# A hybrid decoder layer in float32: a second gate-norm buffer, separate rings for two kinds of tiles, a scratch layout, and an exponential moved

## The chip, the cores and the metric

The kernel runs on one core of one Trainium2 chip. The metric is device time in microseconds of one execution; the times quoted are medians of repeated executions. One further execution was recorded by the hardware profiler; all views of the profile come from that one.

## The reference

One decoder layer (`DEPTH = 1`) works on 1104 token columns: 16 learned meta tokens, 1024 prompt tokens, and 8 sample sequences of 8 tokens. All of it is float32.

```
hn   = rmsnorm(h);  proj = hn @ w_in                       # 1024 -> 4112 columns
ya   = group_rmsnorm(gate_b * conv3(gate_c * hv))          # short convolution, 512 wide
xbc  = silu(conv4(xbc) + b);  xs, B, C = split(xbc)        # 1024 + 256 + 256
dt   = softplus(dt_raw + dt_bias);  a = cumsum(dt * A) per chunk of 128
y    = (C B^T * exp(a_l - a_s), causal) @ (x dt)  +  exp(a) * (C @ state)  +  D * xs
state= exp(a_end) * state + B^T @ (exp(a_end - a) * x dt)  # carried from chunk to chunk
yb   = group_rmsnorm(y * silu(z))                          # 2 groups of 512
h    = h + rmsnorm([ya, yb] @ w_out)
h    = h + rmsnorm((silu(fn @ w_gate) * (fn @ w_up)) @ w_down),  fn = rmsnorm(h)
```

The prompt is one meta chunk and eight chunks of 128; each sample sequence starts from its own recurrent state (8 x 2 x 8 x 64 x 128), which is read, updated and written.

## The kernel before

Every large product is done as three float32r matmuls on split operands (high x high, high x low, low x high). Weights are split on the fly: a transfer into `raw`, a copy on ScalarE (ACT) into the high part, a subtraction on VectorE (DVE) into the low part. `TT` numbers the token tiles: 0 is meta, 1 to 8 the prompt chunks, 9 the samples. Activations that are passed from stage to stage go through DRAM scratch tensors (`d_xbc`, `d_z`, `d_y`, `d_yb`, `d_ya`, `d_h`).

The stages are, in order of time: normalisation and transposes of x; the projections of x, B, C (`px`, until about 216 us); the chunked recurrence with the projections of z and of the short convolution woven between (`ssd_chunk`, `sample_state`, `finish`, `z_rows`, `sconv_rows`, until about 544 us); the output projection (L948 to L984, `o`); gate and up (L1005); down (L1346).

The kernel is written with a framework whose planner lays out each engine's instruction order at build time. It picks among what is ready by priority (program order, moved forward by `tc.high_priority`: 2000 for the chunks, 500 for `finish`, 200 for the samples) and by its own idea of durations; each engine then runs that order strictly, waiting on semaphores. All transfers are issued from the queue of SyncE (SP), in one order too, so a transfer that waits holds back those behind it. A tile with a `tag` has as many buffers as `bufs` says; a new tile of that tag waits until an older one's last reader is done. `po` is the pool of the recurrence; `pf` that of `finish`; `pm`, the pool of the output projection, takes over the memory of `po`: its loads come after the last instructions of `po` in the planned order (`p1.__exit__`, L784; `pmx`, L787).

What the change touches:

- `m_tile` (L384): 5 buffers of 4 KB per partition, tag `M`. They hold the decay matrices of a chunk (two per chunk, L507), the recurrent states of the samples (`s0`, L703, eight tiles, loaded by L706, written back by L728), and some small tiles (`dtmp`, `aT`, `xlo`).
- `y_of` (L483): `E` (one buffer) receives the cumulative log decays broadcast over 64 partitions from `d_a` (L495) and ACT takes the exponential of all of it (L497); DVE uses it in L527. `M` receives decays the same way (L508), has a per-partition value subtracted on DVE or ACT (L513, L516), the exponential on ACT (L517), and a product with `cb` on DVE (L518). `y` (one buffer) is started on ACT (L525) and stored into `d_y` (L539).
- `finish` (L541): loads `d_y` and `d_z` into `yf` and `zt` (one buffer each), gates, normalises, and stores into `d_yb` (L562). Chunk 8 is finished behind `po`'s end (`FIN[9]`, L785), the samples after the last projection (`LATE`).
- `load_mix` (L901): loads `d_yb` (`mrb`) and `d_ya` (`mra`), splits them on ACT (L914) and DVE, for three groups of three token tiles.
- L432 to L444: the cumulative log decays, transposed (`aT`, `aTs`), are stored into `d_a`.

Of the kernel before, what the change touches and what calls it, by code (L numbers as in the profile page):

```python
# [8 lines left out]
F32 = mybir.dt.float32  # L9
F32R = mybir.dt.float32r  # L10
# [6 lines left out]
P = 128  # L17
# [5 lines left out]
NS = 8  # L23
# [32 lines left out]
def hymba_kernel(ctx, tc, x_prompt, x_sample, state_sconv, state_ssm_conv, state_ssm, meta_tokens,  # L56
# [27 lines left out]
    d_xbc = dp.tile([12, P, T], F32, name="d_xbc")  # L84
    d_z = dp.tile([8, P, T], F32, name="d_z")
    d_ya = dp.tile([4, P, T], F32, name="d_ya")
    d_yb = {i: dp.tile([8, P, w], F32, name=f"d_yb{i}") for i, (_, w) in enumerate(TT)}
    d_y = {i: dp.tile([8, P, w], F32, name=f"d_y{i}") for i, (_, w) in enumerate(TT)}
    d_h = {i: dp.tile([w, DM], F32, name=f"d_h{i}") for i, (_, w) in enumerate(TT)}
    d_a = dp.tile([H, NCH + 1, P], F32, name="d_a")  # L90
    d_a2 = {n: dp.tile([P, NF // 2, 512], F32, name=f"d_a{n}") for n in (1, 2, 6, 7, 5, 4, 3)}
    d_fs = dp.tile([NF, 2, P, 32], F32, name="d_fs")
    d_t = dp.tile([P, 4, NF // 2, 512], F32, name="d_t")
# [288 lines left out]


    def m_tile(name):  # L384
        return po.tile([P, 8, P], F32, tag="M", name=name, bufs=5)

    NC2 = NCH + 2
    pd = ps.tile([P, NC2, H], F32, tag="small", name="pd", bufs=NSM)
# [4 lines left out]
        return po.tile([P, NC2, H], F32, tag="sc_" + name, name=name)  # L393

    dt, a_tok, a_end = sc("dt"), sc("a_tok"), sc("a_end")
    tmp = m_tile("dtmp")[:, :, :].rearrange("p j t -> p (j t)")
    t1, t2, t3, da = (tmp[:, q * NC2 * H:(q + 1) * NC2 * H].rearrange("p (c h) -> p c h", h=H) for q in range(4))
    wdt = po.tile([NMETA, 1, H], F32, tag="wdt", name="wdt")
    V.memset(dt, 0.0)
# [29 lines left out]
        V.tensor_tensor(out=e, in0=e, in1=a, op=ALU.subtract)  # L429
        S.activation(e, e, AF.Exp)  # L430
    V.tensor_tensor(out=wdt, in0=a_end[:NMETA, 0:1, :], in1=dt[:NMETA, 0:1, :], op=ALU.mult)
    aT = m_tile("aT")  # L432
    aTs = po.tile([H, NS * LS], F32, tag="soe", name="aTs")
    for c0, n in ((0, 4), (4, 4), (8, 1)):
        pa = ps.tile([P, 4, P], F32, tag="small", name=f"pa{c0}", bufs=NSM)
# [6 lines left out]
            V.tensor_copy(aTs, pa[:H, 0, :NS * LS])  # L442
    SY.dma_start(d_a[:, 0:NCH, :], aT[:H])
    SY.dma_start(d_a[:, NCH, 0:NS * LS], aTs)  # L444
    for j in (10, 11, 0, 1, 2, 3, 4, 5, 6, 7):
        st = xbc_begin(j)
        xbc_history(st)
        for t in range(3):
            xbc_tile(st, t, WIDE)
        xbc_end(st)  # L450
# [32 lines left out]
    def y_of(i, xb, bt, xd, off):  # L483

        t0, w = TT[i]
        c = i - 1
        smp = i > NCH
        if smp:
            E = po.tile([P, 8, NS * LS], F32, tag="ES", name="ES")
            y = po.tile([P, 8, NS * LS], F32, tag="yS", name="yS")  # L490
        else:
            E = po.tile([P, 8, P], F32, tag="E", name=f"E{i}")
            y = po.tile([P, 8, P], F32, tag="y", name=f"y{i}", bufs=YB)
        for e in range(2):
            SY.dma_start(E[64 * e:64 * e + 64, :, :w],  # L495
                         d_a[:, c, :w].rearrange("(j e) t -> e j t", e=2)[e].partition_broadcast(64))
        S.activation(E[:, :, :w], E[:, :, :w], AF.Exp)  # L497
        pcb = ps.tile([P, 2, P], F32, tag="small", name=f"pcb{i}", bufs=NSM)
        cb = po.tile([P, 2, P], F32, tag="cb", name=f"cb{i}")
        mask = U if w == P else Us  # L500
        for g in range(2):
            PE.matmul(pcb[:w, g, :w], xb[:, 8 + g, :w], xb[:, 10 + g, :w], start=True, stop=True)
        V.tensor_tensor(out=cb[:w, :, :w], in0=pcb[:w, :, :w], in1=mask[:w, :w].unsqueeze(1).to_broadcast([w, 2, w]),
                        op=ALU.mult)
        Ms = []
        for g in range(2):
            M = m_tile(f"M{i}{g}")  # L507
            SY.dma_start(M[:w, :, :w], d_a[8 * g:8 * g + 8, c, :w].partition_broadcast(w))  # L508
            mg = M[:w, :, :w]
            for h in range(8):  # L510
                a_s = a_tok[:w, i, 8 * g + h:8 * g + h + 1]
                if g == 0:
                    V.tensor_scalar(out=M[:w, h, :w], in0=M[:w, h, :w], scalar1=a_s, scalar2=0.0,  # L513
                                    op0=ALU.subtract, op1=ALU.min)
                else:
                    S.activation(M[:w, h, :w], M[:w, h, :w], AF.Relu, scale=-1.0, bias=a_s)  # L516
            S.activation(mg, mg, AF.Exp, scale=1.0 if g == 0 else -1.0)  # L517
            V.tensor_tensor(out=mg, in0=mg, in1=cb[:w, g, :w].unsqueeze(1).to_broadcast([w, 8, w]), op=ALU.mult)  # L518
            Ms.append(M)
        if not smp:  # L520
            po_ = big(f"po{i}")
            pov = po_.rearrange("p (j t) -> p j t", j=8)
            off(pov)
        for j in range(8):
            S.activation(y[:, j, :w], xb[:, j, :w], AF.Copy, scale=Dp[:, j:j + 1])  # L525
        if not smp:
            V.tensor_tensor(out=E, in0=pov, in1=E, op=ALU.mult)  # L527
        pd_ = big(f"pd{i}")
        pdv = pd_.rearrange("p (j t) -> p j t", j=8)
        for h in range(H):  # L530
            e = h % 2
            PE.matmul(pdv[64 * e:64 * e + 64, h // 2, :w], xd[:w, h * 64:(h + 1) * 64], Ms[h // 8][:w, h % 8, :w],
                      start=True, stop=True)
        if not smp:
            V.tensor_tensor(out=y, in0=y, in1=E, op=ALU.add)
        V.tensor_tensor(out=y[:, :, :w], in0=pdv[:, :, :w], in1=y[:, :, :w], op=ALU.add)
        if smp:
            return E, y
        SY.dma_start(d_y[i][:, :, :].rearrange("j p t -> p j t"), y)  # L539

    def finish(i):  # L541
        t0, w = TT[i]
        y = pf.tile([P, 8, P], F32, tag="yf", name=f"yf{i}")
        SY.dma_start(y[:, :, :w], d_y[i][:, :, :].rearrange("j p t -> p j t"))
        zt = pf.tile([P, 8, P], F32, tag="zt", name=f"zt{i}")
        SY.dma_start(zt[:, :, :w], d_z[:, :, t0:t0 + w].rearrange("j p t -> p j t"))
        yv = y[:, :, :w]
        V.tensor_tensor(out=yv, in0=yv, in1=zt[:, :, :w], op=ALU.mult)
        sq = zt
        S.activation(sq[:, :, :w], yv, AF.Square)  # L550
        sg = pf.tile([P, 2, P], F32, tag="sg", name=f"sg{i}")
        sv = sq[:, :, :].rearrange("p (g j) t -> p g j t", g=2)[:, :, :, :w]
        V.tensor_tensor(out=sv[:, :, 0:2], in0=sv[:, :, 0:2], in1=sv[:, :, 2:4], op=ALU.add)
        V.tensor_tensor(out=sg[:, :, :w], in0=sv[:, :, 0], in1=sv[:, :, 1], op=ALU.add)
        pn = ps.tile([P, 2, P], F32, tag="small", name=f"pn{i}", bufs=NSM)
        PE.matmul(pn[:, :, :w], ones, sg[:, :, :w], start=True, stop=True)
        S.activation(sg[:, :, :w], pn[:, :, :w], AF.Sqrt, bias=eps_c, scale=0.25 / 512)
        V.reciprocal(sg[:, :, :w], sg[:, :, :w])
        for g in range(2):
            yg = y[:, 4 * g:4 * g + 4, :w]  # L560
            V.tensor_tensor(out=yg, in0=yg, in1=sg[:, g, :w].unsqueeze(1).to_broadcast([P, 4, w]), op=ALU.mult)
        SY.dma_start(d_yb[i][:, :, :].rearrange("j p t -> p j t"), yv)  # L562

    def states(i, bt, xw):
        t0, w = TT[i]
# [120 lines left out]
    def sample_state(u, st):  # L686
# [13 lines left out]
                                in1=mk[h // w], op=ALU.mult)  # L700
            bms[0] = b1, b2
        b1, b2 = bms[0]
        s0 = m_tile(f"s0{u}")  # L703
        for q in range(2):
            rows = slice((j0 + q) * P, (j0 + q + 1) * P)
            SY.dma_start(s0[:, 4 * q:4 * q + 4, :], s_nat[b0:b0 + 4, rows, :].rearrange("b q n -> q b n"))  # L706
# [30 lines left out]
        V.tensor_tensor(out=t, in0=t, in1=E[:, j0:j0 + 2, tl], op=ALU.mult)  # L737
        V.tensor_tensor(out=y[:, j0:j0 + 2, tl], in0=y[:, j0:j0 + 2, tl], in1=t, op=ALU.add)
        if u == NS - 1:
            SY.dma_start(d_y[NCH + 1][:, :, :].rearrange("j p t -> p j t"), y)  # L740

    def conv_states():
        for q in range(2):
            pt = big(f"xlp{q}")
            for j in range(6):
                PE.transpose(pt[0:27, j * P:(j + 1) * P], xlast[:, 6 * q + j, :], ident)
            o = m_tile(f"xlo{q}")[0:27, :, :].rearrange("p j t -> p (j t)")[:, 0:6 * P]
            V.tensor_copy(o, pt[0:27, 0:6 * P])
            sl = slice(q * 6 * P, (q + 1) * 6 * P)
            SY.dma_start(o_xc_s[0].flatten_outer_dims()[:, sl], o[0:24, :])  # L750
            SY.dma_start(o_xc_p[0, 0][:, sl], o[24:27, :])
# [149 lines left out]
    def load_mix(part, tiles):  # L901
        nb = 8 if part == "b" else 4
        for i in sorted(tiles):
            t0, w = TT[i]
            raw = pm.tile([P, nb, P], F32, tag="mr" + part, name=f"mr{part}{i}", bufs=2)
            src = d_yb[i][:, :, :] if part == "b" else d_ya[:, :, t0:t0 + w]
            SY.dma_start(raw[:, :, :w], src.rearrange("j p t -> p j t"))
            mh = pm.tile([P, nb, P], F32R, tag="mh" + part, name=f"mh{part}{i}", bufs=4)
            if w == P:
                ml = pm.tile([P, nb, P], F32R, tag="ml" + part, name=f"ml{part}{i}", bufs=4)  # L910
                lo = ml
            else:
                ml, lo = None, mh[:, :, w:2 * w]
            S.activation(mh[:, :, :w], raw[:, :, :w], AF.Copy)  # L914
            minus(lo, raw[:, :, :w], mh[:, :, :w])
            mix[part, i] = mh, ml
# [496 lines left out]
```

## Time and profile before

| | us |
|---|---|
| median of 3 runs | 1437.35 (1436.61 to 1437.58) |
| profiled execution, its own time | 1438.31 |
| span of the profile | 1436.6 |
| TensorE (PE) busy | 1378.5, 96% of the span |
| VectorE (DVE) busy | 973.1, 68% |
| ScalarE (ACT) busy | 590.5, 41% |
| DMA queue of SP, 16 engines | 52.9% |
| granted TensorE clock, mean | 0.99 |

How to read it: the span begins with the first instruction of the profile and ends with the last; 1.7 us of the execution lie around it. PE is busy nearly everywhere, so what can be had or lost is the time in which PE waits and the time in which its clock is granted at half. The views name a line, an engine and tiles as `out<-in`.

### The profile page before, as it was taken

Reading aid. Unit: us, or ns where it says so; the run is one execution under the profiler, and the core shown is the slowest. Engines: PE = TensorE matmul, PEld = TensorE weight load, DVE = VectorE, ACT = ScalarE, POOL = GpSimd, SP = SyncE. Lnnn points to the kernel's source line nnn. Section 1 sums busy time; section 2 is a strip of 40 time slices with the busy share of each in tenths; the row PEclk is TensorE's granted clock in tenths of the full one; section 3 lists DMA queues with packets and bytes.
Section 4 is the critical chain, followed back from the end, with each engine's and each line's share of the span. In section 5 each row is a group of like instructions: output and inputs, shape, how many; then the busy total and the mean of one; then the engine's idle time right before and its main releaser. Section 6 shows DMA issues by size and latency. Waiting matters only on the chain.

```text
span 1436.6 us, 21982 instructions
## 1 busy us (share of the span) xinstructions
PE 1378.5 (96%) x8837; PEld 1254.4 (87%) x8837; DVE 973.1 (68%) x1321; ACT 590.5 (41%) x939; POOL 57.7 (4%) x110
## 2 busy tenths in 40 slices
PE   6999999989899996999998999999999999999997
PEld 5899998878798985887888999999999998888886
DVE  6455467776777888677489886667676666455565
ACT  5457444344443633466464222223322233443431
POOL 2011000000000000021010000000000000000001
PEclk9999999999999998999999999999999999999999
DMA  7135347666645557775535554443433468655454
GB/s 223 46 102 147 92 127 203 182 174 200 178 120 163 139 148 250 238 239 164 185 111 169 179 178 164 163 171 129 146 114 140 164 204 262 234 189 181 161 173 157
DMA packets 242190, 240.96 MB, mean 168 GB/s; under 512 B 34413, under 2 KB 195265, under 8 KB 242089
## 3 DMA queue, kind: packets, MB, share of 16 engines
q1 hardware_dynamic: 242088, 239.57, 52.9%
q8 instruction: 69, 1.13, 0.3%
q14 instruction: 33, 0.26, 0.1%
HBM read 170.81 MB, written 68.72 MB: 167 GB/s over the span
## 4 chain that ended last, share of the span: by engine, by line
PE 77%; DMA 8%; DVE 7%; ACT 4%; issue 2%; SPq 1%; POOL 0%; DVEq 0%; POOLq 0%; ACTq 0%
PE d L1346 14%; PE o L967 8%; PE yu L1005 7%; PE yg L1005 7%; PE zg L1005 5%; PE zu L1005 5%; PE xu L1005 4%; PE xg L1005 4%; DMA M<-d_a 3%; PE px L207 3%; PE px L209 3%; PE px L208 3%; PE pz L207 1%; DMA out_dram<-s 1%; PE pz L209 1%
## 5 line engine op out<-in xcount | busy, mean ns | idle before, releaser
L207 PE MATMUL px<-xh,whi 128*128 128x448 f32 (+2 forms) x288 | 95.5, 334 | 0.8 <-ACT xr L266 0.8
L208 PE MATMUL px<-xl,whi 128*128 128x448 f32 (+2 forms) x288 | 95.1, 331 | 0.0
L209 PE MATMUL px<-xh,wlo 128*128 128x272 f32 (+2 forms) x288 | 94.7, 332 | 0.0
L96 DVE TENSOR_TENSOR wlo<-raw,whi 128x1024 fp32r<-128x1024 f32 x32 | 39.1, 1221 | 52.3 <-ACT whi L102 45.1
L959 DVE SCALAR_TENSOR_TENSOR wol<-wo,vec,woh 128x1024 fp32r<-128x1024 f32 x36 | 46.1, 1281 | 37.9 <-ACT woh L958 37.9
L207 PE MATMUL pz<-xh,whi 128*128 128x256 f32 (+2 forms) x192 | 64.2, 334 | 2.9 <-DVE z L587 2.9
L209 PE MATMUL pz<-xh,wlo 128*128 128x256 f32 (+2 forms) x192 | 63.7, 332 | 0.0
L208 PE MATMUL pz<-xl,whi 128*128 128x256 f32 (+2 forms) x192 | 63.7, 332 | 0.0
L958 ACT ACTIVATE woh<-wo,vec 128x1024 fp32r<-128x1024 f32 x36 | 41.3, 1149 | 48.7 <-PE o L967 48.7
L239 DVE SCALAR_TENSOR_TENSOR xa<-xr,vec,xa 128x1128 f32<-128x1128 f32 x36 | 50.1, 1391 | 10.9 <-ACT xa L236 10.1
L207 PEld LDWEIGHTS px<-xh,whi 128*128 128x128 f32 x288 | 54.1, 188 | 3.1 <-ACT xr L266 1.0
L1346 PE MATMUL d<-wd,B01h 128*128 128x512 f32 x176 | 54.6, 390 | 2.2 <-ACT wd L1213 1.7
L209 PEld LDWEIGHTS px<-xh,wlo 128*128 128x128 f32 x288 | 54.1, 188 | 2.0 <-issue 0.2
L208 PEld LDWEIGHTS px<-xl,whi 128*128 128x128 f32 x288 | 54.1, 188 | 1.6
L102 ACT ACTIVATE whi<-raw 128x1024 fp32r<-128x1024 f32 x32 | 33.7, 1053 | 48.2 <-PE px L208 30.1
L967 PE MATMUL o<-woh,mhb 128*128 128x512 f32 x144 | 40.9, 407 | 11.8 <-ACT mhb L914 9.3
L967 PE MATMUL o<-wol,mhb 128*128 128x512 f32 x144 | 46.5, 409 | 2.3 <-DVE wol L959 1.9
L1346 PE MATMUL d<-wd,T3h 128*128 128x512 f32 x152 | 46.8, 389 | 0.0
L967 PEld LDWEIGHTS o<-woh,mhb 128*128 128x128 f32 x144 | 27.2, 194 | 19.6 <-ACT mhb L914 9.9
L1346 PE MATMUL d<-wd,T2h 128*128 128x512 f32 x144 | 44.2, 389 | 0.0
L1346 PE MATMUL d<-wd,B11h 128*128 128x512 f32 x144 | 44.0, 389 | 0.0
L967 PE MATMUL o<-woh,mlb 128*128 128x512 f32 x128 | 42.0, 407 | 0.0
(661 smaller groups left out, 4091.4 us busy)
## 6 DMA issues: line engine op xcount, KB each, us to landing
wo<-in_w_out_dram SPq DMA_DIRECT2D x36, 512.0 KB, 3.9
raw<-in_w_in_dram SPq DMA_DIRECT2D x32, 512.0 KB, 4.6
wg<-in_w_gate_dram SPq DMA_DIRECT2D x11, 1024.0 KB, 7.3
wu<-in_w_up_dram SPq DMA_DIRECT2D x11, 1024.0 KB, 6.6
xr<-in_w_down_dram SPq DMA_DIRECT2D x11, 1024.0 KB, 5.1
d_t<-xr SPq DMA_DIRECT2D x11, 1024.0 KB, 4.3
draw<-d_a SPq DMA_DIRECT2D x19, 512.0 KB, 5.0
xt<-in_x_prompt_dram SPq DMA_DIRECT2D x16, 512.0 KB, 5.3
```

The costliest lines, as they stand in the source:

```text
L96: V.tensor_tensor(out=out, in0=a, in1=hi.bitcast(F32), op=ALU.subtract)
L102: S.activation(hi[:, :], raw[:, :], AF.Copy)
L207: PE.matmul(acc, hi[:, wk], xh[t][:, k, o:], start=k == 0, stop=False)
L208: PE.matmul(acc, hi[:, wk], xl[t][:, k, o:], start=False, stop=False)
L209: PE.matmul(acc, lo[:, wk], xh[t][:, k, o:], start=False, stop=k == KD - 1)
L239: V.scalar_tensor_tensor(out=dst, in0=part(row, i), scalar=wv[:, wcol(i):wcol(i) + 1], in1=dst, op0=ALU.mult, op1=ALU.add)
L958: S.activation(hi, raw, AF.Copy, scale=nv)
L959: V.scalar_tensor_tensor(out=lo, in0=raw, scalar=nv, in1=hi[:, :].bitcast(F32), op0=ALU.mult, op1=ALU.subtract)
L967: PE.matmul(accs[i][c], l[:, kb, :], r_[:, c * 512:(c + 1) * 512], start=n == 0 and q == 0, stop=n == 11 and q == len(steps) - 1)
L1005: PE.matmul(acc[:, c, 0:W1], w_[l][k], b[r_][:, k, c * W1:(c + 1) * W1], start=start and k == 0 and x == 0, stop=k == 3 and x == 2, skip_g ...
L1346: PE.matmul(accs[t], sx[x][:, tl], wx[y], start=st and x + y == 0, stop=en and x == 1, skip_group_check=n not in OPENS)
```

## The change

It has four parts. (1) `finish` gets two `yf` buffers; to pay for it, the split short-convolution tiles of the output projection (`mha`, `mla`) get three instead of four. (2) The ring of five becomes `M` with three and `s0` with two; the samples' states and the small tiles go to `s0`. (3) `d_y` and `d_yb` are laid out `[128, 8, w]` instead of `[8, 128, w]`, so that a partition's row of a tile is one run in DRAM (4 KB for w = 128) and not eight runs of 512 bytes. (4) The exponential of the log decays is taken once on 16 partitions, stored into a new scratch tensor `d_e`, and `E` is loaded from there; L497 goes.

```diff
-    d_yb = {i: dp.tile([8, P, w], F32, name=f"d_yb{i}") for i, (_, w) in enumerate(TT)}
-    d_y = {i: dp.tile([8, P, w], F32, name=f"d_y{i}") for i, (_, w) in enumerate(TT)}
+    d_yb = {i: dp.tile([P, 8, w], F32, name=f"d_yb{i}") for i, (_, w) in enumerate(TT)}
+    d_y = {i: dp.tile([P, 8, w], F32, name=f"d_y{i}") for i, (_, w) in enumerate(TT)}
...
+    d_e = dp.tile([H, NCH + 1, P], F32, name="d_e")
...
     def m_tile(name):
-        return po.tile([P, 8, P], F32, tag="M", name=name, bufs=5)
+        return po.tile([P, 8, P], F32, tag="M", name=name, bufs=3)
+
+    def s_tile(name):
+        return po.tile([P, 8, P], F32, tag="s0", name=name, bufs=2)
...
-    tmp = m_tile("dtmp")[:, :, :].rearrange("p j t -> p (j t)")
+    tmp = s_tile("dtmp")[:, :, :].rearrange("p j t -> p (j t)")
...
-    aT = m_tile("aT")
+    aT = s_tile("aT")
...
     SY.dma_start(d_a[:, NCH, 0:NS * LS], aTs)
+    eT = s_tile("eT")
+    S.activation(eT[:H], aT[:H], AF.Exp)
+    S.activation(aTs, aTs, AF.Exp)
+    SY.dma_start(d_e[:, 0:NCH, :], eT[:H])
+    SY.dma_start(d_e[:, NCH, 0:NS * LS], aTs)
...
-                         d_a[:, c, :w].rearrange("(j e) t -> e j t", e=2)[e].partition_broadcast(64))
-        S.activation(E[:, :, :w], E[:, :, :w], AF.Exp)
+                         d_e[:, c, :w].rearrange("(j e) t -> e j t", e=2)[e].partition_broadcast(64))
...
-        SY.dma_start(d_y[i][:, :, :].rearrange("j p t -> p j t"), y)
+        SY.dma_start(d_y[i][:, :, :], y)
...
-        y = pf.tile([P, 8, P], F32, tag="yf", name=f"yf{i}")
-        SY.dma_start(y[:, :, :w], d_y[i][:, :, :].rearrange("j p t -> p j t"))
+        y = pf.tile([P, 8, P], F32, tag="yf", name=f"yf{i}", bufs=2)
+        SY.dma_start(y[:, :, :w], d_y[i][:, :, :])
...
-        SY.dma_start(d_yb[i][:, :, :].rearrange("j p t -> p j t"), yv)
+        SY.dma_start(d_yb[i][:, :, :], yv)
...
-        s0 = m_tile(f"s0{u}")
+        s0 = s_tile(f"s0{u}")
...
-            src = d_yb[i][:, :, :] if part == "b" else d_ya[:, :, t0:t0 + w]
-            SY.dma_start(raw[:, :, :w], src.rearrange("j p t -> p j t"))
-            mh = pm.tile([P, nb, P], F32R, tag="mh" + part, name=f"mh{part}{i}", bufs=4)
+            src = d_yb[i][:, :, :] if part == "b" else d_ya[:, :, t0:t0 + w].rearrange("j p t -> p j t")
+            SY.dma_start(raw[:, :, :w], src)
+            mh = pm.tile([P, nb, P], F32R, tag="mh" + part, name=f"mh{part}{i}", bufs=4 if part == "b" else 3)
...
-                ml = pm.tile([P, nb, P], F32R, tag="ml" + part, name=f"ml{part}{i}", bufs=4)
+                ml = pm.tile([P, nb, P], F32R, tag="ml" + part, name=f"ml{part}{i}", bufs=4 if part == "b" else 3)
```

Left out are the store of the samples' `y` (L740), changed as L539 is, and `xlo` (L747), moved to the second ring as `aT` is.

## Rows read from the trace of the kernel before

**Rows 1.** The page, part 1: busy us (share of the span) and instructions of each engine.
```profile
PE 1378.5 (96%) x8837; PEld 1254.4 (87%) x8837; DVE 973.1 (68%) x1321; ACT 590.5 (41%) x939; POOL 57.7 (4%) x110
```

**Rows 2.** Windows of 36 us: length, busy us of PE, PEld, DVE, ACT, POOL, then PEclk.
```profile
359.00:395.00 36.00, 31.17 (x240) 28.07 (x239) 28.68 (x43) 16.65 (x29) 0.00 (x0) 0.95 0.66 177
...
431.00:467.00 36.00, 35.39 (x227) 32.23 (x226) 26.78 (x29) 11.05 (x17) 1.08 (x2) 1.00 0.57 163
467.00:503.00 36.00, 36.00 (x241) 32.77 (x240) 32.14 (x49) 22.00 (x44) 1.65 (x2) 1.00 0.51 138
...
539.00:575.00 36.00, 25.10 (x102) 20.10 (x101) 29.20 (x29) 13.46 (x18) 0.56 (x1) 0.81 0.79 252
```

**Rows 3.** Waits of PE, 100 to 580 us: total us, times, longest us.
```profile
PE o L967 <- ACT mhb L914: 9.3, 1, 9.3
PE pcb L502 <- ACT bt L469: 4.8, 1, 4.8
PE pz L207 <- DVE z L587: 2.9, 2, 2.4
PE so L732 <- ACT s0t L713: 2.7, 2, 2.1
PE pd L532 <- DVE M L518: 1.4, 2, 1.2
...
PE so L732 <- ACT s0t L711: 0.9, 1, 0.9
```

**Rows 4.** Timeline of ACT: start us, us, instruction, [idle before it <- releaser].
```profile
242.24 1.07 ACT L497 ACTIVATE E<-E 128x1024 f32<-128x1024 f32 x1 [9.60 <-DVE M L513]
...
273.21 1.06 ACT L497 ACTIVATE E<-E 128x1024 f32<-128x1024 f32 x1 [6.40 <-DMA E<-d_a]
...
304.21 2.45 ACT L525 ACTIVATE y<-xb,Dp 128x128 f32<-128x128 f32 x8 [1.39 <-DVE s L725]
...
372.30 2.45 ACT L516 ACTIVATE M<-M,a_tok 128x128 f32<-128x128 f32 x8 [3.19 <-DMA M<-d_a]
```

**Rows 5.** Chain that ended last, in order of time: start us, us, what.
```profile
297.65 6.45 DMA d_y<-y
...
364.14 3.77 DMA out_dram<-s
367.98 4.21 DMA M<-d_a
...
540.74 5.92 DMA d_yb<-yf
...
547.75 6.24 DMA mrb<-d_yb
```

**Rows 6.** DMA issues by tile: count, KB each, median us to landing.
```profile
d_xbc<-xa SPq DMA_DIRECT2D x12, 520.0 KB, 2.7
...
d_y<-y SPq DMA_DIRECT2D x8, 512.0 KB, 6.5
```

**Rows 7.** Timeline of SP's queue, early and at the end of the recurrence.
```profile
97.17 0.38 SPq L443 DMA_DIRECT2D d_a<-aT  x1
...
541.33 0.39 SPq L759 DMA_DIRECT2D out_dram<-fso  x1
546.67 0.36 SPq L544 DMA_DIRECT2D yf<-d_y  x1
547.12 1.96 SPq L907 DMA_DIRECT2D mrb<-d_yb  x2
```

**Rows 8.** Windows at half clock, columns as in rows 2.
```profile
377.70:381.10 3.40, 3.29 (x16) 3.02 (x17) 2.04 (x4) 0.05 (x1) 0.00 (x0) 0.50 0.23 56
...
553.40:558.60 5.20, 5.13 (x12) 3.97 (x13) 4.33 (x7) 2.96 (x5) 0.00 (x0) 0.50 0.62 204
```

**Rows 9.** The samples' states: durations ns, first and last start us.
```profile
L706 SPq DMA_DIRECT2D s<-in_state_ssm_dram x16: 378/506/2268, 112.6 to 387.6; - x16
...
L728 SPq DMA_DIRECT2D out_dram<-s x16: 377/442/1108, 247.3 to 472.5; - x16
```

More of the change, by code (lines that the diff above doesn't have):

```diff
@@ L739, in sample_state @@
         if u == NS - 1:
-            SY.dma_start(d_y[NCH + 1][:, :, :].rearrange("j p t -> p j t"), y)
+            SY.dma_start(d_y[NCH + 1][:, :, :], y)
     def conv_states():
@@ L746, in conv_states @@
                 PE.transpose(pt[0:27, j * P:(j + 1) * P], xlast[:, 6 * q + j, :], ident)
-            o = m_tile(f"xlo{q}")[0:27, :, :].rearrange("p j t -> p (j t)")[:, 0:6 * P]
+            o = s_tile(f"xlo{q}")[0:27, :, :].rearrange("p j t -> p (j t)")[:, 0:6 * P]
             V.tensor_copy(o, pt[0:27, 0:6 * P])
```

## The prediction, made before the result was known

> **What bounds the kernel now.** I read the page's first part, then windows of equal length, the waits of PE, and for each wait the timelines of ACT and SP and the chain. PE is busy 96% of the span [rows 1], so its matmuls are the floor, and none of them changes: only idle time of PE, and time at half clock, can be won. The change touches the stretch from about 100 to 580 us. There the longest wait is 9.3 us, before the first matmul of the output projection; inside the recurrence lie waits of 4.8, 2.9, 2.7, 1.4 and 0.9 us, together 12.7 [rows 3]. Two of the longer waits are followed by a stretch at half clock (0.50, that is 1.2 of 2.4 GHz): 3.3 us of matmuls after the 4.8 us wait, 5.1 after the 9.3 us one [rows 8]. Work at half clock takes twice as long, so these cost about 1.65 and 2.55 us. What the change could win is then at most 12.7 + 1.65 = 14.35 us in the recurrence and 9.3 + 2.55 = 11.85 at its end, 26 together. The reader is also to see how busy DVE is: 28.7 us of 36 in the window of the 4.8 us wait, 32.1 of 36 just after 467 us, where PE has no idle at all [rows 2]. DVE's work does not shrink either.
>
> **Where each wait comes from, and what each part does to it.**
>
> *Separate rings.* In the chain the store of a sample's new state (3.77 us from 364.14) is followed at once by the load of an M (4.21 us from 367.98) [rows 5]: that M took the buffer that the sample's state was leaving. ACT, whose next instruction is the subtraction on this M, idles 3.19 us for it and starts at 372.30 [rows 4]; behind it stand its 2.45 us and one more exponential, and only then the copy `bt` for which PE waits 4.8 us. Without the store in front, the load starts some 3.8 + 0.4 us earlier (the store, and its issue, priced as the 0.38 us of rows 7), so the wait shrinks by 4.2 and its half clock (1.65) goes. The 1.4 us wait for M's product on DVE comes from the same order one step earlier, and I take 1.2 of it. Direct shift: 4.2 + 1.65 + 1.2 = 7.05 us. Ends: 0, if another wait is right behind, and 4.8 + 1.4 + 1.65 = 7.85.
>
> *Exponential of E gone from ACT.* ACT stood idle 9.60 us before the E exponential at 242.24 and 6.40 before that at 273.21 [rows 4]. The first is put down to DVE, but what it reads is the load of E; either way, copies of projections queue behind it, and PE's 2.9 us (longest 2.4) is for `z`, which such a copy feeds. With L497 gone ACT passes on. I take 2.35 of the 2.4 and half of the 0.9 for `s0t`, which follows the second: 2.8 us; ends 0 and 3.3. The wait does not vanish: it moves to DVE's L527, which reads E. Behind L527 in DVE's queue stand the sums into `y` and the splits of weights; it also needs PE's product with the state. If E were as late there as it was for ACT, the 2.8 would be lost. ACT also saves 9 exponentials of up to 1.07 us, worth nothing on an engine that is busy 41% [rows 1].
>
> *y in tile order.* Starting `y` on ACT waits for the store of the last `y`, which lands 297.65 + 6.45 = 304.10 [rows 5]; ACT starts it at 304.21 for 2.45 us [rows 4], and behind it come the `s0t` copies for which PE waits 2.7 [rows 3]. Stores of rows of 512 bytes land after 6.5 us; a store of nearly the same size in long rows, `d_xbc`, after 2.7 [rows 6]. So the store lands up to 3.8 us earlier; I take 2.5 us off PE's wait, since an exponential of M stands before it in ACT's queue. Ends: 0 and 2.7. Loads in long rows may gain too; I put them at nothing. The Trainium skill speaks against this part: "DMA: Bandwidth & Descriptors", Specifications, has runs of 512 bytes already at line rate. By that rule the 2.5 us would be nothing and the sum below 1.5 smaller; no run so far has this tile in long rows, and the two stores above differ by far more than their size.
>
> The direct shifts sum to 7.05 + 2.8 + 2.5 = 12.35 us. I take 60% of it, 7.4: the whole order is laid out anew, and DVE, 28.7 to 32.1 us of 36 [rows 2], has to do the same work in the shorter stretch. The ends stay 0 and 14.35.
>
> *Two yf buffers.* At the end of the recurrence the gated chunk 7 is stored (540.74, landing after 5.92 us) [rows 5]. Chunk 8's load into the one `yf` waits in SP's queue for that landing and is issued at 546.67; directly behind it, at 547.12, go the first loads of the output projection, which need nothing of chunk 7 or 8 [rows 7]. The instruction before them, the store of the final state, was issued at 541.33. With a second buffer chunk 8's load goes right behind (0.39), the projection's loads (0.36 later) at about 542.1: 5.0 us earlier. PE's wait becomes 9.3 - 5.0 = 4.3 us: the final state must still go through PE and ACT before `pm` opens, and the load itself takes 6.24 [rows 5]. A 4.8 us wait left 3.3 us of matmuls at half clock [rows 8], so I keep 1.65 of the 2.55: 0.9 more. Together 5.9; ends 0 (the loads wait for something else of `po`) and 11.85. Late next is that same load and its split.
>
> *What is added.* Two exponentials on 16 partitions (no longer than 1.07 each), two stores (0.38 each in SP's queue), and the first E load, behind these, waits for one of them to land (2.7, as a store of rows 6): some 1.07 + 0.38 + 2.7 = 4.2 us in SP's queue near 100 us, in front of weights for the projections. These are loaded ahead, and PE has no wait of size there (its long ones in rows 3 are later); I put it at 0, ends 0 and 4.2. `mha` and `mla` with three buffers: a group uses three; the fourth only let one split go early. A full-size operation is 1.07 us on ACT [rows 4], half of that for these tiles, and PE works a whole group between load and use: 0, ends 0 and 2.
>
> M with three: the M of the next chunk's second half can be loaded only when this chunk's first eight heads are multiplied. Load 4.21, subtraction 2.45, exponential about 1.06: 7.7 us, against some 36 us from chunk to chunk (the recurrence's last store at 541.33 less the first store of a state at 247.3, over eight) [rows 7, 9]. The old ring was not really wider: eight states were loaded by 387.6 and the last stored at 472.5 [rows 9], so that late in the recurrence states held buffers of the five for long; yet PE lost only 0.6 us of the 36 from 431 [rows 2]. I put it at 0; if its cover is gone, 7.7 a chunk. Two s0 buffers: a state waits for the store of the last but one, a chunk or so back: nothing, or one landing of 3.77.
>
> **Sum.** 7.4 + 5.9 = 13.3 us. The profiled execution took 1438.31 us, so 1425.0; it lies 1.0 above the median of the timed runs, 1437.35, which I take as the base: 1437.35 - 13.3 = 1424.
>
> **The rivals.**
>
> *One half alone.* The recurrence gains nothing that lasts, since DVE then sets the pace, and only the 5.9 us at its end come: 1431.5; the other way round (7.4 alone) 1430. For it: DVE's 32.1 of 36 us. Against: PE's waits lie where DVE had 7 us free.
>
> *Nothing comes of it.* The new order puts another wait where the old ones were (chunk 8's gate, final state), or the loads do not move since they waited for memory of `po`: 1437. For it: all these waits end at transfers of 4 to 6 us, and the planner puts instructions where it believes transfers to be done. Against: at 546.67 and 547.12 nothing but the buffer was in the way.
>
> *Slower: the ring of three.* The planner believes loads to be quick and puts the next chunk's second M right where PE needs it; then ACT and DVE stand at M's load in each chunk, with the fills' copies behind them, as ACT did at 372.30. Of the 7.7 us a third reaching PE in each of 8 chunks is 20.5 us: 1437.35 - 13.3 + 20.5 = 1444.5. It decides from 13.3 / 8 = 1.7 us of PE's wait per chunk. For it: the samples' two M's hold two of the three until their products, so the second M of chunk 1 starts late. Against: rows 2 and 9, as above.
>
> **How the numbers follow.** Forecast 0.55, one half alone 0.20, nothing 0.11, slower 0.14. The measurement can tell 0.2%, 2.9 us, from no change; so faster 0.75, same 0.11, slower 0.14. The likeliest case alone runs from 1414 (nearly all of 26 us) to 1430. The range of 1413 to 1440 takes in the second and third case and leaves out most of the slower one, and little below.
>
> **What would show it.** Right: no ACT instruction on E; loads of M no longer behind a sample's store, and no wait of PE for `bt` or `z` over 1 us; `d_y` landing in 3 to 4 us; the output projection's first loads issued within 1 us of the final state's store, with PE's wait there near 4 us; PE's busy sum the same but for the half clock. Wrong: PE waiting for M or for DVE in most chunks; `E` ending DVE's waits at L527; the first projection load still held by SP's queue.

## The result, and the profile after

The changed kernel takes 1421.42 us (median of 5 runs, 1419.32 to 1423.27) beside 1437.58 us for the kernel before measured with it. The ratio is 0.988, with a 95% interval of 0.9861 to 0.9898: faster by 1.2%, some 16 to 17 us. The forecast was 1424, in a range of 1413 to 1440. The profiled execution took 1421.42 us, with a span of 1419.7.

The engines of the page, as in [rows 1]:

```profile
PE 1376.9 (97%) x8837; PEld 1254.7 (88%) x8837; DVE 972.7 (69%) x1321; ACT 582.9 (41%) x932; POOL 66.1 (5%) x110
```

PE has the same 8837 matmuls and nearly the same busy time. So the 16.9 us of span can lie only in idle time of PE and in time at half clock, and windows cut at the stages say where. First the kernel before, then the changed one; the columns are those of [rows 2], and the stages are the recurrence up to the first matmul of the output projection, then output projection, gate and up, and down.

```profile
216.00:553.40 337.40, 314.41 (x2178) 279.56 (x2176) 261.72 (x352) 141.37 (x256) 7.80 (x16) 0.99 0.61 170
553.40:721.70 168.30, 163.04 (x710) 131.30 (x710) 113.79 (x129) 90.21 (x124) 14.10 (x12) 0.96 0.65 210
721.70:1196.80 475.10, 468.94 (x3721) 467.26 (x3722) 345.08 (x502) 157.79 (x246) 5.00 (x6) 1.00 0.46 158
1196.80:1436.60 239.80, 230.11 (x1014) 189.65 (x1012) 134.17 (x168) 90.30 (x125) 6.68 (x9) 0.99 0.58 195
```

The changed kernel:

```profile
216.00:534.00 318.00, 309.77 (x2151) 275.15 (x2150) 259.50 (x350) 137.95 (x259) 15.83 (x15) 0.99 0.62 179
534.00:700.20 166.20, 161.13 (x736) 131.93 (x735) 114.00 (x130) 87.99 (x123) 15.52 (x14) 1.00 0.65 213
700.20:1178.40 478.20, 471.53 (x3722) 469.59 (x3722) 345.96 (x502) 158.63 (x246) 5.01 (x6) 0.99 0.46 157
1178.40:1419.70 241.30, 231.71 (x1014) 190.74 (x1012) 134.28 (x168) 90.49 (x125) 6.68 (x9) 0.98 0.58 193
```

The length of a window less PE's busy time is PE's idle time. Of a stretch at half clock, half of its matmul time counts as lost. The lengths alone would mislead, because 26 matmuls have moved from the recurrence into the output stage (x2151 for x2178, x736 for x710). By stage, in us:

| stage | idle before | idle after | half clock before | half clock after |
|---|---|---|---|---|
| up to the end of `px` (216) | 14.0 | 13.2 | 0 | 0 |
| recurrence, without the wait for `mhb` | 13.8 | 8.2 | 1.6 | 1.6 |
| wait for `mhb` [rows 3] | 9.3 | 0 | | |
| output projection | 5.3 | 5.1 | 6.0 | 0 |
| gate and up | 6.2 | 6.7 | 1.7 | 4.5 |
| down | 9.7 | 9.6 | 0 | 1.7 |

Four sums follow. The waits inside the recurrence shrank by 5.6. At its end 9.3 + 6.0 + 0.2 = 15.5 went. The two last stages gave 4.9 back (0.5 of idle time less 0.1, and 2.8 + 1.7 of half clock). The first stage gained 0.8. Together 17.0, the difference of the spans (16.9) but for rounding.

All of this is read from one execution of each kernel. The kernel before, timed again beside the experiments, took between 1432.79 and 1444.25 us at mean granted clocks of 0.987 to 0.993, so a few us of half clock in a stage may belong to the execution and not to the kernel.

PE's waits between 100 and 580 us, the four longest; to be held against [rows 3]:

```profile
PE so L740 <- ACT s0t L721: 2.6, 1, 2.6
PE pb L208 <- DVE gc L631: 2.3, 1, 2.3
PE ph L208 <- DVE u L618: 1.5, 2, 1.2
PE pz L208 <- DVE z L595: 1.5, 1, 1.5
```

The waits for `mhb` and for `bt` are gone. The longest near the end is now one of 2.3 us in the short-convolution rows, for `gc`. SP's queue at that place, to be held against [rows 7]:

```profile
522.06 0.39 SPq L767 DMA_DIRECT2D out_dram<-fso  x1
522.54 0.53 SPq L963 DMA_DIRECT2D wo<-in_w_out_dram  x1
523.46 0.79 SPq L570 DMA_DIRECT2D d_yb<-yf  x1
524.30 1.72 SPq L915 DMA_DIRECT2D mrb<-d_yb  x2
```

The final state's store is 19.3 us earlier than before (522.06 for 541.33), and the projection's first loads follow it after 2.2 us instead of 5.8 (547.12). The chain that ended last, from that load on, answers to the end of [rows 5]:

```profile
524.30 6.23 DMA mrb<-d_yb
...
530.55 1.07 ACT mhb L922
```

The load is no faster than before (6.23 for 6.24). What differs is what PE has to do meanwhile, in a window from the final state's transposes to the first `o`:

```profile
520.00:534.00 14.00, 13.65 (x83) 12.60 (x82) 13.54 (x18) 5.75 (x7) 0.06 (x1) 1.00 0.76 228
```

PE is busy for 13.65 of 14.00 us. Of the projections woven into the recurrence, 72 matmuls stand in the timeline between these transposes and the first `o` and 48 more behind it; in the kernel before it was 24 and 24, and then 9.30 us of nothing. The early final state is for the greater part work moved behind it, not time won. The windows from the start to the last of its transposes, before and after:

```profile
0.00:539.73 539.73, 512.00 (x3370) 462.10 (x3371) 368.65 (x514) 249.59 (x444) 31.96 (x83) 1.00 0.53 149
0.00:520.70 520.70, 499.59 (x3297) 450.54 (x3298) 365.66 (x508) 240.00 (x434) 38.80 (x81) 1.00 0.54 155
```

Of the 19.0 us between them, 12.4 are matmuls that now come later (512.00 less 499.59); 6.6 are idle time less.

### The profile page after: what moved, and what is told of

The parts are those of the page before. It is cut to its first block, busy times and chain, and to the rows that moved or that the text cites. A ratio compares the mean times of both kernels' runs of the same rounds, so it can differ in the third digit from the quotient of the medians.

```text
span 1419.7 us, 21974 instructions
## 1 busy us (share of the span) xinstructions
PE 1376.9 (97%) x8837; PEld 1254.7 (88%) x8837; DVE 972.7 (69%) x1321; ACT 582.9 (41%) x932; POOL 66.1 (5%) x110
## 4 chain that ended last, share of the span: by engine, by line
PE 56%; DVE 3%; DMA 2%; ACT 1%; issue 1%; POOL 0%; SPq 0%; DVEq 0%; POOLq 0%; ACTq 0%
PE d L1354 14%; PE o L975 9%; PE yu L1013 7%; PE yg L1013 7%; PE zg L1013 5%; PE zu L1013 5%; PE xg L1013 4%; PE xu L1013 4%; DMA mrb<-d_yb 1%; PE d5s L1365 1%; PE d1s L1365 1%; PE fT L899 1%; DMA drawbh<-in_w_down_dram 0%; DMA d_a<-f 0%; DMA yf<-d_y 0%
## 5 line engine op out<-in xcount | busy, mean ns | idle before, releaser
L524 ACT ACTIVATE M<-M,a_tok 128x128 f32<-128x128 f32 (+1 forms) x72 | 21.8, 384 | 52.8 <-DMA M<-d_a 52.8
L1354 PEld LDWEIGHTS d<-wd,B01h 128*128 128x128 f32 x176 | 33.6, 192 | 10.0 <-ACT wd L1221 2.1
```

The lines of the kernel that those rows point to most:

```text
L1354: PE.matmul(accs[t], sx[x][:, tl], wx[y], start=st and x + y == 0, stop=en and x == 1, skip_group_check=n not in OPENS)
```

## The experiments

All ran beside the kernel before, in five rounds. The changed kernel was timed apart from the others, so all are compared by their ratio to before; "gain" is one minus that ratio, times 1437.58. "Left" counts the projections' matmuls still to come at the final state's transposes, before plus after the first `o`. By the intervals a gain is known to some 2 to 4 us. A profile shows one execution: that of `only_exp`, 1439.58 us, was the longest of twelve.

| kernel | median us | ratio (95%) | gain us | left |
|---|---|---|---|---|
| changed kernel | 1421.42 | 0.988 (0.9861 to 0.9898) | 17.2 | 72 + 48 |
| `no_yf` | 1434.39 | 0.9973 (0.9958 to 0.9989) | 3.9 | 24 + 0 |
| `no_ring` | 1426.02 | 0.991 (0.9891 to 0.9929) | 12.9 | 24 + 24 |
| `no_lay` | 1426.18 | 0.9911 (0.989 to 0.9931) | 12.8 | 72 + 48 |
| `no_exp` | 1425.3 | 0.9914 (0.9895 to 0.9933) | 12.4 | 72 + 48 |
| `only_yf` | 1428.69 | 0.9923 (0.9896 to 0.995) | 11.1 | 24 + 24 |
| `only_ring` | 1437.64 | 0.9989 (0.9971 to 1.0007) | 1.6 | 24 + 0 |
| `only_lay` | 1434.6 | 0.9975 (0.996 to 0.9991) | 3.6 | 24 + 24 |
| `only_exp` | 1434.21 | 0.9967 (0.9954 to 0.9981) | 4.7 | 24 + 0 |
| `yf_ring` | 1429.79 | 0.9945 (0.9929 to 0.9962) | 7.9 | 72 + 48 |
| `b_fill` | 1438.26 | 1.0002 (0.9989 to 1.0016) | -0.3 | 48 + 24 |
| `pool_yf` | 1431.5 | 0.9965 (0.9947 to 0.9982) | 5.0 | 24 + 24 |
| `a_fill` | 1426.25 | 0.9928 (0.9906 to 0.9949) | 10.4 | 72 + 48 |

**One part taken out of the changed kernel.**

`no_yf`: one `yf` buffer again, and four of `mha` and `mla`.

```diff
-        y = pf.tile([P, 8, P], F32, tag="yf", name=f"yf{i}", bufs=2)
+        y = pf.tile([P, 8, P], F32, tag="yf", name=f"yf{i}")
...
```

> The changed kernel with one yf buffer again (and four buffers for the split short-convolution tiles). Theory A (each part removes its own wait, as the prediction priced them): chunk 8's load into yf waits again for the store of chunk 7 and holds the output projection's first loads; PE's wait before that projection comes back, 5.9 us lost: 1427.3 against 1421.4. Theory B (the parts do not stand for themselves: the planner lays the whole order anew and the gain is a property of that order): within 2 us of the changed kernel, or off by an amount with no wait of PE behind yf in the trace.

Measured: 13.3 us of the 17.2 are lost. SP's queue at the end of the recurrence:

```profile
546.79 0.39 SPq L767 DMA_DIRECT2D out_dram<-fso  x1
547.75 0.32 SPq L552 DMA_DIRECT2D yf<-d_y  x1
548.13 1.37 SPq L915 DMA_DIRECT2D mrb<-d_yb  x2
```

The queue does not hold the projection's loads here for long (1.34 us behind the final state's store). The final state itself is 24.7 us later than in the changed kernel (546.79 for 522.06). And PE does not wait for `mhb`, but for the short convolution:

```profile
PE pb L208 <- DVE gc L631: 5.9, 2, 5.3
```

So here the second buffer is worth more than twice the 5.9 us of the prediction, and not by the stall on SP's queue alone: with it the planner ends the recurrence earlier, in part by leaving more projections behind it (120 for 24).

`no_ring`: one ring of five for both.

```diff
-        return po.tile([P, 8, P], F32, tag="M", name=name, bufs=3)
+        return po.tile([P, 8, P], F32, tag="M", name=name, bufs=5)
     def s_tile(name):
-        return po.tile([P, 8, P], F32, tag="s0", name=name, bufs=2)
+        return m_tile(name)
```

> The changed kernel with one ring of five for M, states and small tiles again. Theory A: loads of M stand again behind stores of the samples' states; ACT waits for them with copies for PE behind, 4.2 us lost (the priced 7.05 at 60%): 1425.6, at most 1428.5. Theory B: no such rise; ACT waits for M in either kernel, and PE has projections to do meanwhile: 1420 to 1423.

Measured: 4.3 us lost. The expected size comes out, but by another way: PE waits 2.0 us for `bt`, and 3.7 for `mhb`, since only 24 matmuls are left to cover that load.

`no_lay`: `d_y` and `d_yb` as `[8, P, w]`, with the rearranged views, at all five places.

```diff
-        SY.dma_start(d_y[i][:, :, :], y)
+        SY.dma_start(d_y[i][:, :, :].rearrange("j p t -> p j t"), y)
...
```

> The changed kernel with y and yb in DRAM as eight blocks of 128 partitions again (runs of 512 bytes). Theory A: stores of y land later again and ACT's start of the next y with them: 1.5 us lost, 1422.9. Theory B: the store is not on PE's path in the new order: 1421.4 within 1 us, with only the landings of d_y and d_yb longer.

Measured: 4.4 us lost; neither size fits. The landings stand further below.

`no_exp`: `E` from `d_a`, with the exponential on ACT, and without the five lines on `eT` and `d_e`.

```diff
-                         d_e[:, c, :w].rearrange("(j e) t -> e j t", e=2)[e].partition_broadcast(64))
+                         d_a[:, c, :w].rearrange("(j e) t -> e j t", e=2)[e].partition_broadcast(64))
+        S.activation(E[:, :, :w], E[:, :, :w], AF.Exp)
...
```

> The changed kernel with the exponential of E on ACT again, no d_e. Theory A: ACT idles again before E with copies of projections behind: 1.7 us lost, 1423.1, at most 1424.5. Theory B: 1421.4 within 1 us. Both expect ACT busy longer by some 8 us.

Measured: 4.8 us lost, nearly three times its term (60% of 2.8, 1.7). The three losses of 4 to 5 us look alike, though the parts have nothing in common. Whether a mere re-order stands behind them is asked at `a_fill` below.

**One part added to the kernel before.** Each has the diff of its part above, turned round, and nothing else.

> The kernel before with the second yf buffer alone (and three buffers for the split short-convolution tiles). Taken out of the changed kernel it cost 13 us, not the 5.9 priced, and there chunk 6 came 16 us later and the final state 24 us later in order, although PE waited little in between. Theory C (the single buffer sets the order: the planner, holding loads of the next chunk behind yf's load, puts chunks 6 to 8 later and projections earlier, so that none are left to cover the start of the output projection): most of the gain alone, 1424 to 1429, with chunk 6's store of y well before the 464 us of before. Theory A (only SP's wait of 5 us): 1431 to 1433, chunk 6 where it was. Theory D (the parts only work together): 1435 or more.

`only_yf` gains 11.1 us alone. Its rows at the end of the recurrence are what the prediction had worked out for this step. SP's queue:

```profile
541.18 0.38 SPq L762 DMA_DIRECT2D out_dram<-fso  x1
541.66 3.17 SPq L910 DMA_DIRECT2D mrb<-d_yb  x2
```

and PE's wait:

```profile
PE o L970 <- ACT mhb L917: 4.7, 1, 4.7
```

The loads go out at 541.66 (predicted 542.1) and the wait is 4.7 us (predicted 4.3). In the profiled execution, 7.6 us shorter in span than before, more than the 5.9 is to be seen: half clock in the output stage falls by 3.4 us (6.0 to 2.6), not 0.9, and other waits of the recurrence by 4.4. Its recurrence does lose 4.8 more to half clock, and gate and up 3.0. Its final state comes no earlier than before (541.18 for 541.33).

> The kernel before with the two rings alone. Theory A: the 7.05 us of direct shifts at 60%, 4 to 7 us gained: 1430.5 to 1433.5, no wait of PE for bt. Theory C: with one yf buffer the end of the recurrence stays where it was and the gain is 0 to 4: 1433.5 to 1437.5.

`only_ring`: its interval includes no change. The wait for `bt` is gone from PE's list, and these are its longest waits now:

```profile
PE pb L207 <- DVE gc L626: 5.9, 2, 5.3
PE so L735 <- ACT s0t L716: 2.8, 1, 2.8
PE ph L207 <- DVE u L613: 2.5, 1, 2.5
```

The wait for `mhb` is gone too, although there is one `yf` buffer; other waits took their place, at the recurrence's end above all 5.3 us for `gc`, which DVE makes.

> The kernel before with the DRAM layout of y and yb alone. Theory A: 1.5 to 2.5 us gained: 1435 to 1436. By the changed kernel without it, which lost 4.3 us: 1433.

> The kernel before with the exponential taken once alone. Theory A: 1.7 to 2.8 us gained: 1434.7 to 1435.8, no idle of ACT before E. By the changed kernel without it, which lost 3.4 us: 1434.

`only_lay` gains 3.6 us and `only_exp` 4.7. Alone the four parts sum to 11.1 + 1.6 + 3.6 + 4.7 = 21.0 us; taken out they sum to 13.3 + 4.3 + 4.4 + 4.8 = 26.8; together they give 17.2. They do not add up. Which differences can be put down to a part is asked behind `a_fill`.

The layout has a direct test, since its price was the time to landing. The DMA issues, last column the median us to landing; in the changed kernel:

```profile
d_y<-y SPq DMA_DIRECT2D x8, 512.0 KB, 5.3
...
d_yb<-yf SPq DMA_DIRECT2D x8, 512.0 KB, 2.9
mrb<-d_yb SPq DMA_DIRECT2D x8, 512.0 KB, 4.6
```

In `no_lay`, the old layout in the changed kernel's order:

```profile
d_y<-y SPq DMA_DIRECT2D x8, 512.0 KB, 5.6
...
d_yb<-yf SPq DMA_DIRECT2D x8, 512.0 KB, 3.1
```

In `only_lay`, the new layout and all else as before:

```profile
d_y<-y SPq DMA_DIRECT2D x8, 512.0 KB, 5.4
...
d_yb<-yf SPq DMA_DIRECT2D x8, 512.0 KB, 7.6
```

These medians rest on the one to three stores whose landing the trace shows. `d_yb` lands in 7.6 us with rows of 4 KB, and in 3.1 with runs of 512 bytes: it is the order of the work that sets its landing; by what was not taken apart. The layout itself is worth 0.2 to 0.3 us of it between the first two. For `d_y` it is 6.5 before [rows 6], 5.4 with the layout alone.

**What makes the end so large.**

`yf_ring`: the second `yf` buffer and the two rings, with the old layout and the old exponential.

> The kernel before with two of the four parts: second yf buffer (three buffers for the split short-convolution tiles) and the two rings; layout and exponential as before. Alone they gave 11 and under 2 us. Theory E (these two together make the planner end the recurrence early, with projections left to cover the start of the output projection; the other two parts only shorten waits): 1424 to 1428, over 100 projection matmuls behind the final state's copy (46 and 24 when alone), no wait of PE for mhb over 1 us. Theory F (that early end needs all four): 1427 to 1430, a wait for mhb of some 4 us.

Measured: 120 matmuls are left at the final state, as in the changed kernel, and PE's list has no wait for `mhb`. These are its longest waits:

```profile
PE pb L207 <- DVE gc L626: 3.3, 2, 2.9
PE pc L207 <- DVE gc L626: 3.2, 1, 3.2
```

So these two parts together, and neither alone (24 + 24 and 24 + 0 left), bring the early final state. Yet its gain of 7.9 is smaller than that of `only_yf`, 11.1, though the intervals touch: the order alone does not make the time.

`b_fill`: is it only the cover? The kernel before, with one row of projections fewer handed out before the final state.

```diff
-FILL = [2, 2, 2, 3, 2, 2, 2, 2, 3]
+FILL = [2, 2, 2, 3, 2, 2, 2, 2, 2]
```

> The kernel before with one edit alone: the last entry of FILL is 2 and not 3, so that one more projection step is left to come behind the recurrence. Nothing of the change is in it. Theory G (what the end of the recurrence is worth is a matter of cover: PE has too few projections there): 24 more matmuls stand before the first of the output projection, some 4 us of PE's 9.3 us wait are covered: 1431 to 1434. Theory A (it takes the buffer): yf's load still holds the loads, the covering matmuls only move: 1437 within 2 us.

Measured: no gain (1.0002).

```profile
PE pcb L502 <- ACT bt L469: 4.9, 1, 4.9
PE pb L207 <- DVE gc L623: 3.7, 3, 2.9
PE o L967 <- ACT mhb L914: 3.5, 1, 3.5
```

24 more matmuls cover part of the load, and the wait for `mhb` falls from 9.3 to 3.5 us. Of these 5.8 us 3.2 come back as other idle time, 2.9 of them for `gc` behind the first `o`: recurrence and output projection together idle 25.8 us instead of 28.4. In this execution 2.6 us more are lost there at half clock (10.2 for 7.6). Cover that is only moved there gains nothing by itself. Nor is an earlier final state what the buffer needs: `only_yf` gained 11.1 without one.

`pool_yf`: is it SP's queue? One `yf` buffer (and four of `mha` and `mla`, as in `no_yf`), but its loads (except the meta and sample tiles') go out from POOL's queue, where they hold back none of SP's.

```diff
-        y = pf.tile([P, 8, P], F32, tag="yf", name=f"yf{i}", bufs=2)
-        SY.dma_start(y[:, :, :w], d_y[i][:, :, :])
+        y = pf.tile([P, 8, P], F32, tag="yf", name=f"yf{i}")
+        (G if w == P else SY).dma_start(y[:, :, :w], d_y[i][:, :, :])
...
```

> The changed kernel with one yf buffer again, as in no_yf (1434.4), but the load of yf for the eight chunks is issued from the queue of GpSimd, so that it waits there and holds nothing in SP's queue. Theory A (the single buffer costs by holding SP's queue): close to the changed kernel, 1422 to 1426. Theory H (the single buffer itself makes the gates follow one another, in the plan and on the chip, whichever queue waits): 1430 to 1435.

Measured: a gain of 5.0 over before, some 1.1 more than `no_yf` and inside its interval; 12.2 short of the changed kernel.

```profile
PE o L975 <- ACT mhb L922: 5.7, 1, 5.7
```

The final state is 8.1 us earlier than in `no_yf` (its store at 538.72), but PE waits for `mhb` again. The held queue explains a small part at most of what `no_yf` lost, where it had held the loads for 1.34 us only. These loads land no later from POOL's queue (2.6 to 4.6 us) than in the changed kernel (2.6 to 5.8). The buffer itself, and what the planner does with it, is the rest; which of the two is not shown.

`a_fill`: a control. The changed kernel, with the edit of `b_fill`, which adds and removes no work.

> The changed kernel with the last entry of FILL 2 and not 3, nothing else. The order of the last projections against the recurrence moves a little; no work, buffer or transfer changes. A measure of what a new order alone is worth: 1421.4 within 2 us, and if one more step of cover still helps there, up to 2.3 us less, PE's wait behind the recurrence.

Measured: 6.8 us slower than the changed kernel by the ratios (0.9928 for 0.988), 4.6 by the medians. PE idles 3.0 us more in the recurrence and 2.0 more in the output projection. Two of its waits:

```profile
PE pb L208 <- DVE gc L631: 3.9, 1, 3.9
PE pz L208 <- DVE z L595: 2.8, 1, 2.8
```

A mere re-order can cost as much as taking out a part, though the same edit cost the kernel before nothing (`b_fill`). So where the order of the instructions changes with the part, a difference of that size cannot be put down to the part. That holds for the rings: taking them out cost 4.3 us, adding them gained 1.6 alone, and with the second buffer they took 3.2 away (`yf_ring` beside `only_yf`).

It does not hold for the layout. In the traces every engine of `no_lay` runs its instructions in the order of the changed kernel, and every engine of `only_lay` in the order of the kernel before; `no_exp` and `yf_ring`, which differ by the layout alone, share one order too. These three pairs differ by 4.4, 3.6 and 4.5 us with no re-order behind them. For the exponential it holds in part: its instructions differ, but PE's matmuls stand at the same places but for 4 of 8837 in the changed kernel and `no_exp` (4.8 us), and in `no_lay` and `yf_ring` (4.9 us). In other orders the two parts brought less, 1.8 us together from `only_yf` to `no_ring` and 2.3 from `only_ring` to `no_yf`.

The effect of the `yf` buffer is 13.3 and 12.2 us taken out (`no_yf`, `pool_yf`) and 11.1 alone, which is above what the re-order moved, but 6.3 where only the rings are there too (`only_ring` to `yf_ring`), which is not.

## Why the prediction was right or wrong

The time was right: 13.3 us forecast, 16.2 between the medians. PE's matmuls as the floor, the 26 us that could be had, and the sign of both halves hold. But the sum came out by errors that offset each other (1.8 us too much in the recurrence, 9.6 too little at its end, 4.9 given back later), and that is luck.

**The recurrence: 7.4 predicted, 5.6 measured.** The 60% taken of the direct shifts was near as a sum, but not in its parts: the rings had 4.2 us of it and are not shown to bring anything, while the layout (1.5) and the exponential (1.7) brought more, as told below. The rings' mechanism is shown: no load of M stands behind a sample's store any more. SP's wait before and after, first the kernel before (total, times, longest us):

```profile
SPq L508 <- DMA out_dram<-s: 12.7, 6, 5.4
```

and the changed kernel:

```profile
SPq L516 <- PE pd L540: 16.4, 7, 6.2
SPq L714 <- DMA out_dram<-s: 13.8, 6, 3.7
```

The samples' own loads (L714) now wait for the stores, and the loads of M (L516) wait for the products of the ring of three. In `no_ring` the wait of M's loads for those stores is back (13.2 us). `bt` is gone from PE's waits. That this gained 7.05 us is not shown: alone, the rings gave 1.6, with an interval that includes no change. The wait for `z` fell from 2.9 to 1.5 us, not under 1, and that for `s0t` (L713, now L721) from 2.7 to 2.6, where the layout and the exponential had been given 2.5 and 0.45.

**Two yf buffers: 5.9 predicted, 15.5 at that place. This term is the step that failed**, by its size. Its own working holds in `only_yf` (541.66 and 4.7 us for 542.1 and 4.3), which yet gained 11.1. Two things were missed. First, the order is laid out anew as a whole, so the second buffer does not only let two loads pass SP's queue: in `only_yf` PE's other waits in the recurrence shrank too, by 4.4 us (that for `bt` from 4.8 to 2.2). With the rings it brought the final state forward by 19 us with 120 of the projections' matmuls left instead of 48, and then the load was covered entirely. The prediction had kept the planned order as it was and put "late next" the load and its split, a wait of 4.3. Second, the half clock behind the wait was priced at 2.55, and only 0.9 of it as won; the stage lost 6.0 in three stretches, and all of it went. How much of the 6.0 was the wait's is not shown: the third stretch begins at 678, 125 us behind it, and in `only_lay`, with the order of before and a wait of 7.9 us at that place, the stage lost 1.9. Nor does the gain hang on the early final state: `yf_ring` has it and gained 7.9, `only_yf` (11.1) and `no_ring` (12.9) do not.

**Not foreseen: 4.9 us given back in the profiled execution.** The gate, up and down stages, which the change does not touch, lose 4.5 us more to half clock and idle 0.4 more. That the change does this is not shown (last section). One of the three stretches of the changed kernel, in the down stage (the first is shown in the last section):

```profile
1187.20:1190.60 3.40, 3.40 (x9) 2.63 (x9) 3.40 (x4) 2.31 (x3) 0.00 (x0) 0.50 0.95 202
```

**The layout.** "`d_y` landing in 3 to 4 us" was wrong (5.3). The term compared a store with another of a different moment, `d_xbc`, and took the difference for the layout's. The Trainium skill, "DMA: Bandwidth & Descriptors", Specifications, which has runs of 512 bytes already at line rate, was the better guide to the landing: with the order held, the two stores land in 5.6 and 3.1 us with runs of 512 bytes and in 5.3 and 2.9 with runs of 4 KB. The very store that was priced (6.45 us from 297.65) lands in 5.4 in `only_lay`. By that rule the part would be worth nothing, and there the measurement differs: with the order held it is worth 3.6 to 4.5 us, where the prediction had 1.5. In `only_lay` PE's waits for `s0t`, which the prediction had named, fall from 2.7 + 0.9 [rows 3] to

```profile
PE so L735 <- ACT s0t L716: 1.3, 1, 1.3
```

ACT starts the `y` behind that store at 301.38 instead of 304.21; 1.1 us of this is the landing, and the rest it had gained before, at `E` (271.46 for 273.21). So the forecast mechanism is there, as the smaller part; where the rest comes from is not shown.

**The exponential.** `E` ends no wait of ACT any more, and PE never waits for it. But ACT's idle time went to M, in the changed kernel:

```profile
ACT M L524 <- DMA M<-d_a: 52.8, 9, 8.6
```

before:

```profile
ACT E L497 <- DMA E<-d_a: 25.0, 5, 9.1
ACT M L516 <- DMA M<-d_a: 23.3, 6, 6.1
```

The 52.8 us for M alone are about the 25.0 + 23.3 for E and M before. On an engine busy 41% of the time this need not reach PE, and the part is worth 4.8 and 4.9 us at nearly the same order, where the prediction had 1.7; which wait of PE pays it is not shown.

**The slower rival** had the ring of three hold up ACT, and it does: nine such stops, the longest 8.6 us. Its other half failed, that a third would reach PE: PE's list has no wait for M, so the point of 1.7 us a chunk was never reached. **One half alone** put the buffer alone at 1431.5 (gain 5.9; measured 11.1), and the recurrence alone at 1430 (gain 7.4; measured 3.9 in `no_yf`). **Of the signs to look for**, two more: the first loads followed the final state's store after 2.2 us, not within 1, and PE's wait there was 0, not 4.

**What stays open.** Why the planner, given both the buffer and the rings, ends the recurrence 19 us earlier, when the queue alone (`pool_yf`) and the cover alone (`b_fill`) do not do it. Its costs and due times were not taken apart; chunk 6 of the eight gives one sign, its `d_y` store, which is issued at 447.14 in the changed kernel, 464.31 before and 453.8 in `yf_ring`. Also open is the worth of the rings, below what a re-order moves, and how the layout brings some 4 us when its stores land at most 1.1 us sooner at the same order.

## What to carry to other kernels

When a planner lays out the whole order, price a freed buffer by its stall only as a first estimate, and ask what the planner will move with it: here the buffer alone gained 11.1 us, while the wait that it was priced by shrank by 4.6. Before a part of a change is judged by taking it out, compare the order of the instructions with and without it. Where it is the same, as with the layout here, the difference is the part's; where it is not, measure what a neutral re-order does to the same kernel (6.8 us here) and put no smaller difference down to the part. And compare transfers at the same place in the same order: a landing of 7.6 or 3.1 us told of two orders of the work, not of the layout.

## What the runs showed of the hardware that was not expected

Nearly the same pause of PE is followed by half clock in one kernel and not in the other. At the first pause of gate and up, the slice with the pause and the one behind it, in the changed kernel:

```profile
712.80:716.20 3.40, 1.51 (x10) 1.04 (x11) 1.67 (x3) 2.64 (x6) 1.92 (x2) 0.99 0.26 106
716.20:723.00 6.80, 6.11 (x29) 5.71 (x28) 3.93 (x3) 1.92 (x4) 0.08 (x1) 0.50 0.78 235
```

and in the kernel before:

```profile
734.10:737.50 3.40, 1.73 (x12) 1.02 (x10) 2.12 (x4) 2.36 (x6) 1.56 (x2) 1.00 0.12 49
737.50:740.90 3.40, 2.78 (x22) 2.65 (x23) 1.96 (x2) 1.71 (x3) 0.00 (x0) 1.00 0.61 185
```

PE was busy for 1.51 us of the slice in the one and 1.73 in the other; the clock then stood at 0.50 (1.2 GHz) for 6.8 us and at 1.00 (2.4 GHz). Over the gate, up and down stages 16.3 us of idle time went with 6.2 us lost at half clock after, 15.8 with 1.7 before. The change is not shown to be the cause. In the fourteen kernels profiled, whose edits all leave these stages alone, they idle 14.8 to 16.7 us and lose 1.5 to 6.3 at half clock. `no_exp` and `yf_ring`, which have one order on every engine, lose 1.7 and 4.7. So a difference of a few us at half clock between two single profiles is not yet an effect of a change; no run here shows how to steer it.
